# Where the softmax rows of a chunk-attention kernel are normalised: VectorE or ScalarE for the two longer query tiles

## The chip, the cores and the metric

The kernel runs on one core of a Trainium2 chip. The metric is the device time of one execution in microseconds (us), as the median of several runs. A core has several engines that work side by side, each with its own queue of instructions: TensorE (PE in the profile; its weight loads are listed apart as PEld), VectorE (DVE), ScalarE (ACT), GpSimd (POOL) and SyncE (SP), which here only issues DMAs. Each queue is worked off in order; engines wait for one another with semaphores.

## The reference

An input x of 512 frames by 1024 channels goes through two residual layers. Layer 0 has a pooling mixer, layer 1 chunked attention; both are followed by a gated MLP with a causal convolution of width 3. All sub-layers begin with an RMSNorm. What matters here is the attention of layer 1, with 16 heads of 64 channels:

```python
qkv = h @ w_qkv
q, k, v = jnp.split(qkv, 3, axis=-1)
q = head_rmsnorm(q.reshape(B, S, N_HEADS, HEAD_DIM), q_norm)
k = head_rmsnorm(k.reshape(B, S, N_HEADS, HEAD_DIM), k_norm)
...
s = jnp.einsum('bqhd,bkhd->bhqk', qc, kb).astype(jnp.float32) * scale + bias[None]
...
p = jax.nn.softmax(s, axis=-1).astype(vb.dtype)
return jnp.einsum('bhqk,bkhd->bqhd', p, vb)
```

A chunk has 64 frames, and a frame attends to its own chunk and the eight before it, which in a sequence of 512 frames means all earlier chunks and its own.

## The kernel before

All data is float32, and every large matrix product is made of three products of split operands: a value is split into a rounded part (hi, written by ACT with a Copy) and the remainder (lo, a subtraction on DVE, or on POOL where the code asks for it). The helper `split` at lines 91 and 92 does that, `split_scaled` at 96 and 97 the same with a scale, and `mm3` at 112 to 114 issues the three products. Profile rows with L91, L92 or L112 to L114 therefore come from many places; their tile names tell which.

The program is a row of stages: the pooling mixer, the MLP of layer 0 (until about 380 us), the attention (about 380 to 650 us), the MLP of layer 1. PE's order is written out by hand in the attention (`manual_schedule` for PE alone). On the other engines the order is not written out: a planner in the compiler lays the instructions of each queue by times that it works out itself, and so it may place everything anew when an instruction changes its engine.

The attention loop walks over 64 steps: 16 heads h times 4 tiles t of 128 query rows. Because of the causal chunks, tile t only needs the first (t+1) x 128 keys, so tiles 0 to 3 have 128, 256, 384 and 512 columns. Step i does this in PE's order:

- `scores(h, t)` for step i: two matmuls (L661, L662) into PSUM; DVE adds the bias and takes the row minimum of the negated scores (L665); ACT takes the exponential with its row sum (L667); DVE takes the reciprocal of the sum (L668); and the row is multiplied with the reciprocal. For t of 2 and 3 DVE does that (L670, a tensor_scalar), for t of 0 and 1 ACT (L672, a Copy with a scale column).
- `turn(h, t)` for the tile two steps back (LAG is 2): PE transposes the normalised rows (L680, tile tp), then ACT and DVE split the result into the tiles pt.
- `mix(h, m)` two steps later again: the products with V (L695), which ACT and DVE gather into O2 (L699, L700, tile o).
- In two of eight steps `channel_major` for the next pair of heads: transposes of Q or K (L632), then a split on ACT and DVE (L96, L97, or L636 and L639, tile kl), and moves by DMA.

Between these, PE is filled with "fillers": the projections of Q and K for later heads (tile qk), later the output product (tile wo). At the end of each projection a burst of other work comes: ACT reads four PSUM tiles twice (L587, L588), DVE reduces the squares (L589), works out the norm (L590 to L593, tiles qk_a, qk_t, qk_y), and POOL multiplies the four tiles z with it (L595). The split of the weights for fillers has its lo half on POOL (tiles wqk_l and wo_l in L92). POOL also issues the DMA that loads the bias tile B of each head (L655) and writes a corner of it (L656).

When two heads are done, their O2 is split as input of the output product (tile names two<-o). The tiles sb that hold the rows exist four times, as do the small tiles mx for minimum, sum and reciprocal.

Of the kernel before, what the change touches and what calls it, by code (L numbers as in the profile page):

```python
# [19 lines left out]
AF = mybir.ActivationFunctionType  # L20
OP = mybir.AluOpType
# [45 lines left out]
def trunk(ctx: ExitStack, tc: tile.TileContext, xt, xT, cols, band, edge, poolw, gv, wout, wqk, wv, wo, rel, out):  # L67
    nc = tc.nc
# [14 lines left out]
    def psum(tag, name, bufs=2):  # L83
        return ps.tile([P, S], F32, name=name, tag=tag, bufs=bufs)
# [459 lines left out]
    def attention():  # L544
# [103 lines left out]
        def scores(h, t):  # L648

            p, e = divmod(h, 2)  # L650
            q, k, kl = QK[p, 0][e], QK[p, 1][e], KL[p % 2][e]
            if t == 0:
                BT[h] = B = big.tile([P, S], F32, name=f"B{h}", tag="B", bufs=2)
                base = rdram[h, :]
                nc.gpsimd.dma_start(B, bass.AP(tensor=base.tensor, offset=base.offset, ap=[[1, P], [1, S]]))  # L655
                nc.gpsimd.memset(B[:HD, :HD], -NEG)  # L656
            n = (t + 1) * P
            nw = max(n, 256)

            sc = psum("S", f"sc{h}_{t}", 4)  # L660
            nc.tensor.matmul(sc[:, :nw], q[:, t * P:n], k[:, :nw], start=True, stop=False)  # L661
            nc.tensor.matmul(sc[:, :nw], q[:, t * P:n], kl[:, :nw], start=False, stop=True)  # L662
            SM[h, t] = s_ = big.tile([P, S], F32, name=f"sb{h}_{t}", tag="sb", bufs=4)
            mx = tmp.tile([P, 3], F32, name=f"mx{h}_{t}", tag="mx", bufs=4)
            nc.vector.tensor_tensor_reduce(out=s_[:, :n], in0=sc[:, :n], in1=BT[h][:, :n][:, ::-1], scale=1.0,  # L665
                                           scalar=3e38, op0=OP.add, op1=OP.min, accum_out=mx[:, 0:1])
            nc.scalar.activation(s_[:, :n], s_[:, :n], AF.Exp, scale=-1.0, bias=mx[:, 0:1], accum_out=mx[:, 1:2])  # L667
            nc.vector.reciprocal(mx[:, 2:3], mx[:, 1:2])  # L668
            if t > 1:
                nc.vector.tensor_scalar(s_[:, :n], s_[:, :n], mx[:, 2:3], None, op0=OP.mult)  # L670
            else:
                nc.scalar.activation(s_[:, :n], s_[:, :n], AF.Copy, scale=mx[:, 2:3])  # L672

        def turn(h, t):

# [39 lines left out]
        with tc.manual_schedule(engines={mybir.EngineType.PE}):  # L715
# [17 lines left out]
            for i in range(nb + LAG + LAGM):  # L733
                steps = []
                if i < nb:
                    steps.append(lambda: scores(*tiles_[i]))
                if i % 8 in CM and i // 8 + 1 < NPAIR:
                    steps.append(lambda: channel_major(i // 8 + 1, CM.index(i % 8)))
                j = i - LAG
                if 0 <= j < nb:  # L740
                    steps.append(lambda: turn(*tiles_[j]))
                j2 = j - LAGM
                if 0 <= j2 < nb and j2 % 2:
                    steps.append(lambda: mix(tiles_[j2][0], tiles_[j2][1] // 2))
                for x, step in enumerate(steps):
                    step()
                    fill(i + (x + 1) / len(steps))

                while 8 * kept + 7 <= j2 and (cur == 3 or cur == 2 and done >= 24 * (kept // 2 + 1)):
                    split(O2[kept], XS[kept], XS[KD + kept])  # L750
                    kept += 1
# [65 lines left out]
```

## Time and profile before

| | |
|---|---|
| median of 3 runs | 1012.05 us (1011.98 to 1012.12) |
| the profiled execution: time | 1011.85 us |
| the profiled execution: span of its instructions | 1010.1 us |
| mean granted clock of PE in it | 0.997 |
| PE idle from 460 to 640 us | 15.8 us (180.00 less 164.19) |

The span is the time from the first to the last instruction of the program; some 1.8 us of the execution lie around it. The profile's tables are read like this. A row of a timeline has the start in us, the duration in us, the engine, the line of the kernel, the operation, the tiles out<-in, the shape, how many were merged, and in brackets the idle time of the engine before it with what ended that. A row of a group ends in busy us, the mean in ns, and the idle time before. A row of the windows view has, for one stretch of the span, the length and then the busy us of each engine with its count of instructions, then the granted clock of PE (1.00 is full), the share of time in which the DMA engines were busy and GB/s. A row of the waits view has who waited for whom, the us in total, how often, and the longest. The page shows PE's clock and the DMA in 40 slices:

```profile
PEclk9999999999999999999999999999999999999999
DMA  7222323332332234243343333312232342332323
```

Read with the first part of the page, which shows PE nearly always busy, this says that DMA traffic is far from its limit over the whole span.

### The profile page before, as it was taken

The numbers are of one execution on the slowest core, as the hardware profiler recorded it, in microseconds if no ns is written. First come the engines' busy times: TensorE is split into PE (matmuls) and PEld (weight loads), VectorE is DVE, ScalarE is ACT, GpSimd is POOL, SyncE is SP. The second block draws the span as 40 slices with busy tenths as digits, with TensorE's granted clock in tenths as the row PEclk, the third lists the DMA queues.
The fourth block names the chain that finished last, engine by engine and source line by source line (L and its number), as shares of the span: only waits on it lengthen the run. The fifth ranks groups of instructions, "written<-read, shape, count | busy, mean of one in ns | idle before, by whom it ended". The sixth has DMA issues, their size and how long they took to land.

```text
span 1010.1 us, 15577 instructions
## 1 busy us (share of the span) xinstructions
PE 982.3 (97%) x5906; PEld 866.4 (86%) x5906; DVE 820.2 (81%) x1430; ACT 533.5 (53%) x920; POOL 116.4 (12%) x119
## 2 busy tenths in 40 slices
PE   8899999999999999999998889999999999999998
PEld 8678999999999988888777677878999999999986
DVE  7799999988898754443888799989999998989843
ACT  6655544544454443345785767646545454454521
POOL 2400000000000013104524242130000000000000
PEclk9999999999999999999999999999999999999999
DMA  7222323332332234243343333312232342332323
GB/s 288 84 85 82 116 85 109 99 125 95 100 104 82 78 100 146 86 124 115 110 120 83 106 86 92 104 63 97 90 115 98 99 131 90 100 105 86 108 71 112
DMA packets 37290, 105.29 MB, mean 104 GB/s; under 512 B 4416, under 2 KB 6864, under 8 KB 37088
## 3 DMA queue, kind: packets, MB, share of 16 engines
q1 hardware_dynamic: 35728, 99.77, 31.2%
q0 software_dynamic: 1312, 4.24, 1.6%
q8 instruction: 46, 0.75, 0.3%
q10 hardware_dynamic: 176, 0.30, 0.1%
q14 instruction: 28, 0.23, 0.1%
HBM read 95.86 MB, written 2.14 MB: 97 GB/s over the span
## 4 chain that ended last, share of the span: by engine, by line
PE 86%; DVE 8%; ACT 3%; issue 2%; DMA 1%; DVEq 0%; SPq 0%; ACTq 0%
PE out L113 8%; PE out L112 8%; PE out L114 8%; PE st_t L113 6%; PE st_t L112 6%; PE st_t L114 6%; PE st_b L113 5%; PE st_b L112 5%; PE st_b L114 5%; PE gv L113 3%; PE gv L114 3%; PE gv L112 3%; PE qk L114 3%; PE qk L112 3%; PE qk L113 3%
## 5 line engine op out<-in xcount | busy, mean ns | idle before, releaser
L91 ACT ACTIVATE g_h<-gv_r 128x1024 fp32r<-128x1024 f32 x68 | 57.7, 848 | 81.7 <-PE st_t L113 41.0
L113 PE MATMUL out<-one,ow_h 128*128 128x512 f32 x224 | 88.0, 393 | 0.0
L112 PE MATMUL out<-one,ow_h 128*128 128x512 f32 x224 | 87.8, 392 | 0.0
L114 PE MATMUL out<-one,ow_l 128*128 128x512 f32 x224 | 87.7, 392 | 0.0
L91 ACT ACTIVATE ow_h<-wo_r 128x640 fp32r<-128x640 f32 (+1 forms) x64 | 50.5, 789 | 65.2 <-PE out L113 47.3
L511 DVE TENSOR_TENSOR X<-out,X 128x512 f32<-128x512 f32 (+1 forms) x65 | 44.1, 679 | 40.6 <-PE out L114 40.2
L112 PE MATMUL st_t<-h,g_h 128*128 128x256 f32 x272 | 76.9, 283 | 0.0
L114 PE MATMUL st_t<-h,g_l 128*128 128x256 f32 x272 | 76.9, 283 | 0.0
L113 PE MATMUL st_t<-h,g_h 128*128 128x256 f32 x272 | 76.9, 283 | 0.0
L114 PE MATMUL st_t<-two,g_l 128*128 128x256 f32 x272 | 76.5, 281 | 0.0
L113 PE MATMUL st_t<-two,g_h 128*128 128x256 f32 x272 | 76.4, 281 | 0.0
L112 PE MATMUL st_t<-two,g_h 128*128 128x256 f32 x272 | 76.2, 280 | 0.0
L91 ACT ACTIVATE g_h<-sa 128x1024 fp32r<-128x1024 f32 x34 | 36.1, 1060 | 60.2 <-PE st_t L113 42.8
L92 DVE TENSOR_TENSOR g_l<-gv_r,g_h 128x1024 fp32r<-128x1024 f32 x68 | 64.7, 951 | 2.7 <-ACT g_h L91 2.2
L92 DVE TENSOR_TENSOR ow_l<-wo_r,ow_h 128x640 fp32r<-128x640 f32 (+1 forms) x64 | 56.6, 885 | 1.3 <-ACT ow_h L91 1.2
L112 PE MATMUL st_b<-h,g_h 128*128 128x256 f32 x204 | 57.7, 283 | 0.0
L114 PE MATMUL st_b<-h,g_l 128*128 128x256 f32 x204 | 57.7, 283 | 0.0
L113 PE MATMUL st_b<-h,g_h 128*128 128x256 f32 x204 | 57.6, 283 | 0.0
L114 PE MATMUL st_b<-two,g_l 128*128 128x256 f32 x204 | 57.4, 281 | 0.0
L113 PE MATMUL st_b<-two,g_h 128*128 128x256 f32 x204 | 57.3, 281 | 0.0
L112 PE MATMUL st_b<-two,g_h 128*128 128x256 f32 x204 | 57.1, 280 | 0.0
L354 DVE SCALAR_TENSOR_TENSOR c<-a,col,c 128x511 f32<-128x511 f32 (+1 forms) x76 | 56.3, 743 | 0.1
(319 smaller groups left out, 3146.1 us busy)
## 6 DMA issues: line engine op xcount, KB each, us to landing
gv_r<-gv SPq DMA_DIRECT2D x88, 512.0 KB, 3.6
wo_r<-wout SPq DMA_DIRECT2D x32, 384.0 KB, 3.1
wo_r<-wout SPq DMA_DIRECT2D x32, 320.0 KB, 2.9
wqk_r<-wqk SPq DMA_DIRECT2D x16, 512.0 KB, 3.6
wv_r<-wv SPq DMA_DIRECT2D x8, 512.0 KB, 3.5
B<-rdram POOLq DMA_DIRECT2D x16, 256.0 KB, 3.7
wo_r<-wo SPq DMA_DIRECT2D x8, 512.0 KB, 3.5
z<-zh SPq DMA_DIRECT2D x24, 128.0 KB, 2.4
```

The source lines that it names most:

```text
L91: nc.scalar.activation(hi, raw, AF.Copy)
L92: return (eng or nc.vector).tensor_sub(lo, raw, hi.bitcast(F32))
L112: yield nc.tensor.matmul(o, sh, mh, start=first, stop=False)
L113: yield nc.tensor.matmul(o, sh, ml, start=False, stop=False)
L114: yield nc.tensor.matmul(o, sl, mh, start=False, stop=last)
L354: nc.vector.scalar_tensor_tensor(c[:, j:], a[:, :S - j], cw[2 - j], c[:, j:], op0=OP.mult, op1=OP.add)
L511: nc.vector.tensor_add(X[d][:, fs], o[:, fs], X[d][:, fs])
```

## The change

The branch on the tile goes: the multiplication with the reciprocal is a Copy with a scale column on ACT for all four tiles. The reciprocal stays on DVE.

```diff
             nc.scalar.activation(s_[:, :n], s_[:, :n], AF.Exp, scale=-1.0, bias=mx[:, 0:1], accum_out=mx[:, 1:2])
             nc.vector.reciprocal(mx[:, 2:3], mx[:, 1:2])
-            if t > 1:
-                nc.vector.tensor_scalar(s_[:, :n], s_[:, :n], mx[:, 2:3], None, op0=OP.mult)
-            else:
-                nc.scalar.activation(s_[:, :n], s_[:, :n], AF.Copy, scale=mx[:, 2:3])
+            nc.scalar.activation(s_[:, :n], s_[:, :n], AF.Copy, scale=mx[:, 2:3])
```

That is 32 instructions, 16 of 128 x 384 and 16 of 128 x 512 elements, which pass from DVE's queue to ACT's.

## The prediction

> **What bounds the kernel now.** I read the first part of the page, then the windows view cut into the kernel's stages, to see which engine the time belongs to and whether the changed stage holds anything to win.
>
> ```profile
> PE 982.3 (97%) x5906; PEld 866.4 (86%) x5906; DVE 820.2 (81%) x1430; ACT 533.5 (53%) x920; POOL 116.4 (12%) x119
> core 0: us, PE busy (x) PEld busy (x) DVE busy (x) ACT busy (x) POOL busy (x), PEclk, DMA share, GB/s
> 460.00:640.00 180.00, 164.19 (x912) 134.05 (x911) 143.31 (x387) 127.68 (x322) 60.73 (x56) 0.98 0.35 100
> 640.00:730.00 90.00, 89.13 (x447) 75.49 (x447) 85.91 (x130) 52.48 (x79) 12.32 (x7) 1.00 0.28 93
> ```
>
> PE is the bound: 982.3 of 1010.1 us. The softmax steps lie between 460 and 640, and there PE is busy for 164.19 of 180.00, so 15.8 us are idle; DVE has 80% and ACT 71% of the stretch. PE's order is written by hand, so an idle microsecond that goes here goes from the end, unless something behind is late. In the 90 us behind, PE is busy for 89.13; DVE is at 95% there, but its inputs are the sums that the last attention products give, so it moves up with them.
>
> Next, the timelines of DVE and POOL at the largest hole, and that of PE at the four holes that end on a softmax tile.
>
> ```profile
> 569.33 0.49 DVE L670 TENSOR_SCALAR sb<-sb,mx 128x512 f32<-128x512 f32 x1
> 507.25 0.42 DVE L670 TENSOR_SCALAR sb<-sb,mx 128x384 f32<-128x384 f32 x1
> 532.57 6.17 DVE L670 TENSOR_SCALAR sb<-sb,mx 128x512 f32<-128x512 f32 x1
> 582.45 3.78 DVE L670 TENSOR_SCALAR sb<-sb,mx 128x512 f32<-128x512 f32 x1
> 603.22 1.73 DVE L670 TENSOR_SCALAR sb<-sb,mx 128x512 f32<-128x512 f32 x1
> 628.98 1.49 DVE L670 TENSOR_SCALAR sb<-sb,mx 128x512 f32<-128x512 f32 x1
> 532.11 4.04 POOL L595 TENSOR_TENSOR z<-z,qk_y 128x512 f32<-128x512 f32 x4
> 536.11 2.33 POOL L92 TENSOR_TENSOR wqk_l<-wqk_r,wqk_h 128x1024 fp32r<-128x1024 f32 x1
> 539.00 0.55 PE L680 MATMUL tp<-ident,sb 128*128 128x128 f32 x3 [3.94 <-DVE mx L665]
> 586.49 0.66 PE L680 MATMUL tp<-ident,sb 128*128 128x128 f32 x4 [1.78 <-DVE mx L665]
> 605.10 0.63 PE L680 MATMUL tp<-ident,sb 128*128 128x128 f32 x4 [0.69 <-DVE sb L670]
> 630.62 0.63 PE L680 MATMUL tp<-ident,sb 128*128 128x128 f32 x4 [0.46 <-DVE sb L670]
> ```
>
> This is what the changed line costs. L670 takes 0.49 us for 512 columns, but one of them takes 6.17: it starts at 532.57, while POOL is multiplying, and ends at 538.74, 0.3 us after POOL's unbroken run of products and split (536.11 plus 2.33). The others with holes behind them have the same picture. So L670 stands still while POOL works, and everything behind it on DVE with it; the transposes of the softmax tile come late. The releaser that the first two rows name, L665, is the next instruction in DVE's queue, which stood behind the same L670.
>
> **The change, part by part.** It takes 32 instructions L670 from DVE and puts 32 Copies with a scale column on ACT, one per tile of query rows 2 and 3. Reciprocals stay. No DMA is issued or moved. Prices come from the groups by form in 460 to 640, and the clock and the bursts from finer windows:
>
> ```profile
> L670 DVE TENSOR_SCALAR sb<-sb,mx 128x512 f32<-128x512 f32 x16 | 21.3, 1330 | 0.4
> ...
> L670 DVE TENSOR_SCALAR sb<-sb,mx 128x384 f32<-128x384 f32 x16 | 7.7, 482 | 0.3
> ...
> L672 ACT ACTIVATE sb<-sb,mx 128x256 f32<-128x256 f32 x16 | 8.0, 502 | 1.2 <-DVE mx L668 1.2
> ...
> L672 ACT ACTIVATE sb<-sb,mx 128x128 f32<-128x128 f32 x16 | 6.3, 396 | 4.1 <-DVE mx L668 4.0
> 520.00:530.00 10.00, 8.25 (x43) 5.92 (x42) 9.57 (x24) 8.89 (x23) 2.52 (x2) 1.00 0.46 131
> 539.00:545.00 6.00, 6.00 (x27) 5.15 (x28) 3.56 (x11) 4.24 (x12) 0.00 (x0) 0.72 0.27 90
> 565.00:570.00 5.00, 4.92 (x29) 3.44 (x27) 4.72 (x13) 5.00 (x13) 0.56 (x1) 1.00 0.45 126
> 570.00:575.00 5.00, 2.33 (x13) 1.62 (x13) 4.86 (x9) 4.16 (x12) 2.51 (x2) 1.00 0.38 89
> 575.00:580.00 5.00, 4.01 (x13) 2.76 (x13) 3.91 (x14) 2.86 (x9) 0.00 (x0) 0.73 0.33 107
> 590.00:640.00 50.00, 47.10 (x278) 38.82 (x279) 45.94 (x131) 38.85 (x102) 11.31 (x12) 1.00 0.33 96
> ```
>
> Removed from DVE: 21.3 + 7.7 = 29.0 us. Undisturbed it would be 16 x 0.49 + 16 x 0.42 = 14.6, so about 14.4 us are standing still. What counts is the part that PE lost: 3.94 + 1.78 + 0.69 + 0.46 = **6.87 us**. The first hole has a second price: in the 6 us behind it PE has a mean clock of 0.72, and 0.28 x 6 = **1.7 us**. PE stayed busy on the full clock behind the shorter holes at 605 and 630, so I credit this to the long hole and take it as gone. Together 8.6 us.
>
> What is late next at these holes? The same tile's Copy on ACT. ACT's row before it and PE's last matmul before the hole decide:
>
> ```profile
> 531.84 1.05 ACT L91 ACTIVATE wqk_h<-wqk_r 128x1024 fp32r<-128x1024 f32 x1
> 534.66 0.40 PE L113 MATMUL qk<-wqk_l,two 128*128 128x512 f32 x1
> 510.96 0.49 PE L680 MATMUL tp<-ident,sb 128*128 128x128 f32 x3
> ```
>
> At the first hole ACT is free at 532.89, a Copy would end near 533.6, and PE comes for the tile at 535.06: covered by 1.4 us. At the two last holes the tile steps follow each other faster and the margin is smaller: PE lost only 0.69 and 0.46 us to a DVE instruction stretched by 1.2 and 1.0, so the tile's room was some 0.5 us, and a Copy that waits no longer than that closes them too.
>
> Added to ACT: L672 shows 396 ns for 128 columns and 502 for 256, which is 106 per 128 more. Carried on (an estimate from these two rows) that is 0.61 us for 384 and 0.71 for 512, and 16 x 0.61 + 16 x 0.71 = **21.2 us** of work. How much of it delays PE no row shows; the bounds are 0, as long as ACT is idle or the tile has time, and 21.2. Three kinds of place:
> - From 460 to about 590, outside the bursts, the tile has time: the L670 that began at 507.25 ended at 507.67, and its transposes ran at 510.96. A Copy that is 0.2 us longer and queues for one or two more is hidden by those 3.3 us. I take 0.
> - In the bursts, where a projection ends and ACT must read four PSUM tiles twice, ACT has 8.89 of 10 us and 5.00 of 5. Two Copies, 1.3 us, come on top, three times. DVE is relieved of 0.9 us in the same place and is itself at 9.57 of 10. I take 0.7 each, 2.0 us, between 0 and 1.3 each.
> - From 590 on, 12 Copies are 7.9 us, and ACT goes from 38.85 to about 46.8 of 50, that is 94%; DVE falls from 45.94 (12 of the L670, two of them stretched, 7.6 us) to about 38. The two engines change places, and PE lost 2.9 us there with DVE at 92%. Of these, 1.15 are counted above. I take 0.7 us more than now, between 0 and 7.9.
>
> Sum: 8.6 won, 2.7 given back, **5.9 us** less. The profiled execution took 1011.85 us with a span of 1010.1; 1011.85 - 5.9 = 1005.95. The median of 1012.05 is 0.2 above it, so I say **1006.0**.
>
> The Trainium skill has a rule against this change: its page "ScalarE: Activation LUTs" (Rules for kernel authors) puts plain multiplications on VectorE rather than ScalarE. The rows bear that out for one instruction alone, 0.49 us against an estimated 0.71 at 512 columns. By that rule the change would lose 21.2 - 14.6 = 6.6 us where both are on the path, and 1011.85 would become 1018.5; the sum above differs because the row with 6.17 is the same multiplication standing still.
>
> **The rivals.**
> *The load costs nothing and the bursts gain too.* The chain at 571 runs over DVE, which is 4.86 of 5 us busy there:
>
> ```profile
> 569.73 0.74 DVE L639 SCALAR_TENSOR_TENSOR kl<-zt,gq,zh 64x512 fp32r<-64x512 f32 x1
> 571.39 0.35 PE L661 MATMUL sc<-z,z 128*128 128x256 f32 x1 [1.43 <-DVE kl L639]
> ```
>
> L670 stands right before the L639 for which PE waits, so up to 0.4 us goes in each of two bursts, and if the holes at 570 to 577 shrink, the second stretch of slow clock (0.27 x 5 = 1.35 us) goes with them. Then 1012.05 - 8.6 - 0.8 - 1.35 = 1001.3. Against it: ACT is full at that place.
>
> *The standing still moves to another DVE instruction.* Other DVE work meets POOL as well:
>
> ```profile
> L590 DVE TENSOR_TENSOR qk_a<-qk_s,r 128x32 f32<-128x32 f32 x3 | 5.0, 1673 | 0.0
> L92 DVE TENSOR_TENSOR two<-o,two 128x512 fp32r<-128x512 f32 x7 | 4.8, 682 | 0.0
> ...
> L593 DVE TENSOR_TENSOR qk_y<-qk_y,n_y 128x32 f32<-128x32 f32 x3 | 0.5, 182 | 0.0
> ```
>
> L590 and L593 have the same size, and L590 takes nine times as long. The split of the attention output (two<-o) could be caught in the same way if DVE's new order puts it into POOL's run of 4.04 + 2.33 us; none of the 7 is caught now. Price: a hole like that at 535 again, 3.94 + 1.7 = 5.6 us, so 1006.0 + 5.6 = 1011.6. The Trainium skill, "SBUF — State Buffer" (Who interferes with whom), says that a DVE instruction with two SBUF inputs contends with a POOL instruction that reads SBUF, and that the later one waits for the whole of the other; L590 with 1673 ns agrees. By that rule the two<-o split is exposed, and the Copies on ACT are not.
>
> *ACT becomes the bound, and the kernel is slower.* The place is 590 to 640 and the bursts. ACT's queue is in order, and a Copy waits at its head for the reciprocal on DVE; behind it stand the next tile's exponential and the halves of the transposed tiles, for which DVE and PE wait.
>
> ```profile
> ACT sb L672 <- DVE mx L668: 5.2, 10, 1.2
> ```
>
> The 32 Copies of now lost 5.2 us to that wait; as much again, with 7.9 us of late work and 4.0 in the bursts, is 17.1 us if PE sees all of it: 1012.05 - 8.6 + 17.1 = 1020.6. It decides from 8.6 us on, half of that. For it: 94% of ACT's time from 590 on. Against it: DVE at 92% in that same stretch lost PE under 3 us.
>
> **How the numbers follow.** A measurement of this kernel tells about 0.2%, 2 us, from no change, so "same" is 1010.0 to 1014.1. The forecast, 1002.5 to 1010: 0.64. Load free and bursts better, under 1002.5: 0.15. Standing still moved, or half of the ACT load on the path, 1010 to 1014: 0.12. ACT the bound, above 1014: 0.09. Faster 0.79, same 0.12, slower 0.09. The range takes in the free load from 1001.3 and the moved stall up to 1011.6: **1001.0 to 1012.0**.
>
> **What would show it.** Right: in 460 to 640 PE's idle time falls from 15.8 to about 10 us; no hole of over 2 us in front of a transpose; one stretch of slow clock at most; the Copies have means near 0.61 and 0.71; DVE falls by some 25 to 29 us there and ACT rises by about 20. Wrong: a DVE instruction of over 3 us in the stretch, another than L670, means that the stall moved; many waits of transposes or of L91 for ACT after 590 mean that ACT took the bound; a PE idle time that falls while the span doesn't means that the next stage, with DVE at 95%, was late.

## The result, and the profile after

The changed kernel takes 1005.34 us (median of 6 runs, 1004.67 to 1007.35) against 1011.98 us (6 runs, 1011.68 to 1012.12): a ratio of 0.994, interval 0.9927 to 0.9952. That is 6.6 us less, where 5.9 were forecast. The profiled execution took 1005.48 us with a span of 1003.7, 6.4 us less than the span before.

The first part of the page after:

```profile
PE 980.1 (98%) x5906; PEld 867.8 (86%) x5906; DVE 796.7 (79%) x1398; ACT 549.7 (55%) x952; POOL 115.5 (12%) x119
```

The windows view of the same two stages as before; the softmax stage now ends at 634, and the 90 us behind it begin there:

```profile
core 0: us, PE busy (x) PEld busy (x) DVE busy (x) ACT busy (x) POOL busy (x), PEclk, DMA share, GB/s
460.00:634.00 174.00, 162.78 (x915) 136.00 (x914) 120.36 (x356) 144.39 (x354) 59.79 (x56) 0.97 0.37 105
634.00:724.00 90.00, 89.13 (x448) 75.70 (x449) 85.94 (x129) 52.11 (x79) 12.30 (x7) 1.00 0.30 93
```

The stage is 6 us shorter. PE's idle time in it falls from 15.8 us to 174.00 - 162.78 = 11.2, and its busy time by 1.4. DVE loses 143.31 - 120.36 = 23.0 us and ACT gains 16.7 (the window is 6 us shorter too). The next stage hides nothing and takes nothing: 89.13 of 90.00, as before. So nearly the whole gain, 6.0 of 6.4 us, comes from where it was looked for. What is left of the idle time is not where it was looked for.

The groups by form in the softmax stage, with busy us and mean ns behind the bar:

```profile
L669 ACT ACTIVATE sb<-sb,mx 128x512 f32<-128x512 f32 x16 | 11.4, 716 | 0.3 <-DVE mx L668 0.3
L669 ACT ACTIVATE sb<-sb,mx 128x384 f32<-128x384 f32 x16 | 9.8, 609 | 0.6 <-DVE mx L668 0.5
```

The waits view of the stage: who waits for whom, us in total, how often, the longest:

```profile
PE tp L677 <- ACT sb L669: 8.9, 6, 3.3
```

And PE's timeline at the two longest of these waits:

```profile
527.65 1.11 PE L677 MATMUL tp<-ident,sb 128*128 128x128 f32 x4 [3.34 <-ACT sb L669]
572.84 0.66 PE L677 MATMUL tp<-ident,sb 128*128 128x128 f32 x4 [2.71 <-ACT sb L669]
```

The Copies (L669 now) cost 716 and 609 ns, 21.2 us in all. The hole of 3.94 us that L670 had made is gone, and no DVE instruction in the stage lasts over 2 us. But the transposes of the softmax tile (L677 now) wait 8.9 us for the Copy, and two of these waits are 3.34 and 2.71 us long. Both come before the four transposes of a 512-column tile, both at a projection's end. The timelines of ACT, DVE and POOL ahead of the first one show the chain:

```profile
518.40 0.68 DVE L665 CUSTOM_DVE_ANT_0 sb<-sc,B 128x512 f32<-128x512 f32 x1
522.45 1.14 ACT L91 ACTIVATE wqk_h<-wqk_r 128x1024 fp32r<-128x1024 f32 x1
523.66 0.81 ACT L667 ACTIVATE sb<-sb,mx 128x512 f32<-128x512 f32 x1
523.75 2.35 POOL L92 TENSOR_TENSOR wqk_l<-wqk_r,wqk_h 128x1024 fp32r<-128x1024 f32 x1
524.32 1.82 DVE L590 TENSOR_TENSOR qk_a<-qk_s,r 128x32 f32<-128x32 f32 x1
526.49 0.15 DVE L668 RECIPROCAL mx<-mx 128x1 f32<-128x1 f32 x1
526.89 1.00 ACT L669 ACTIVATE sb<-sb,mx 128x512 f32<-128x512 f32 x2
```

The minimum of the row is there at about 519.1, but the exponential runs at 523.66, behind the burst's squares and copies and the weight split of 1.14 us. Its sum is ready at about 524.6; by then DVE is inside L590, which lies beside POOL's weight split and takes 1.82 us. The reciprocal follows at 526.49, the Copy at 526.89, and PE, which had finished at 524.3, begins at 527.65. ACT's queue, DVE's queue and POOL's split beside it stand in a row here, and the Copy itself is the shortest part. In the kernel before, ACT's timeline has the same exponential 3.5 us earlier, 2.0 us after its minimum:

```profile
520.18 0.78 ACT L667 ACTIVATE sb<-sb,mx 128x512 f32<-128x512 f32 x1
```

So the planner's new order of ACT's queue, and not the length of the Copies, is the longest part of the chain.

The windows view around this hole shows PE's clock behind it:

```profile
524.00:527.00 3.00, 0.31 (x2) 0.00 (x0) 2.97 (x7) 2.95 (x11) 2.10 (x1) 0.82 0.22 47
527.00:530.00 3.00, 2.35 (x8) 2.06 (x9) 2.04 (x9) 2.09 (x5) 0.00 (x0) 0.50 0.62 189
530.00:533.00 3.00, 3.00 (x13) 2.62 (x11) 1.71 (x6) 0.78 (x2) 2.20 (x3) 0.54 0.00 0
```

In the 6 us that follow, the granted clock is 0.50 and 0.54, as it was below full behind the largest hole of before.

### The profile page after: what moved, and what is told of

It is laid out like the page before. It is cut to its first block, busy times and chain, and to the rows that moved or that the text cites. A ratio compares the mean times of both kernels' runs of the same rounds, so it can differ in the third digit from the quotient of the medians.

```text
span 1003.7 us, 15609 instructions
## 1 busy us (share of the span) xinstructions
PE 980.1 (98%) x5906; PEld 867.8 (86%) x5906; DVE 796.7 (79%) x1398; ACT 549.7 (55%) x952; POOL 115.5 (12%) x119
## 4 chain that ended last, share of the span: by engine, by line
PE 86%; DVE 6%; ACT 5%; DMA 1%; issue 1%; SPq 0%; DVEq 0%; ACTq 0%
PE out L113 8%; PE out L112 8%; PE out L114 8%; PE st_t L113 6%; PE st_t L112 6%; PE st_t L114 6%; PE st_b L113 5%; PE st_b L112 5%; PE st_b L114 5%; PE gv L113 3%; PE gv L114 3%; PE gv L112 3%; PE qk L114 3%; PE qk L112 3%; PE qk L113 3%; PE oo L692 2%
```

## The experiments

Two questions were open. Was it the standing still of L670 that the change removed, or simply DVE's load? And what did the 21.2 us of Copies cost? Times are medians; each ratio is to the kernel before, run beside it, with its interval in brackets. The kernel before had medians of 1011.88 to 1012.14 us in these runs, and single runs from 1010.63 to 1015.51, so two kernels whose intervals overlap are not told apart by their medians.

### The multiplication stays on DVE, in a form that isn't held up

From the kernel before; the second operation adds zero, and the row's sum goes to a column that nobody reads:

```diff
-            mx = tmp.tile([P, 3], F32, name=f"mx{h}_{t}", tag="mx", bufs=4)
+            mx = tmp.tile([P, 4], F32, name=f"mx{h}_{t}", tag="mx", bufs=4)
...
-                nc.vector.tensor_scalar(s_[:, :n], s_[:, :n], mx[:, 2:3], None, op0=OP.mult)
+                nc.vector.tensor_scalar(s_[:, :n], s_[:, :n], mx[:, 2:3], 0.0, op0=OP.mult, op1=OP.add, accum_out=mx[:, 3:4])
```

> The kernel before, with the 32 multiplications left on DVE, but as a tensor_scalar that also writes its row sum (unused). Theory A (the gain is that DVE no longer stands still behind POOL): if this form does not stand still, the holes of PE at 535, 582, 603 and 628 close although DVE has more work (estimated from 128x384 and 128x512 DVE rows of 0.55 and 0.69 us and accumulator reads of 0.08: 7.8 us more than undisturbed), so 1004 to 1008 us, and no L670 longer than 1 us. Theory B (the gain is that DVE, at 92% from 590 on, lost 14.6 us of work): DVE gets fuller, so 1012 to 1016 us. If the form stands still as well, L670 again has a maximum of several us and the time is 1012 or more, and A and B are not told apart by it.

Measured: **1001.03 us**, 0.9889 [0.9872, 0.9906], the lowest median of all kernels here, and 3 us below the range that theory A gave. The groups by form of this kernel:

```profile
L670 DVE TENSOR_SCALAR_CACHE_REDUCE sb<-sb,mx 128x512 f32<-128x512 f32 x16 | 11.9, 742 | 0.4
L670 DVE TENSOR_SCALAR_CACHE_REDUCE sb<-sb,mx 128x384 f32<-128x384 f32 x16 | 9.8, 610 | 0.3
```

Its timeline of POOL and DVE where one of them meets POOL:

```profile
531.01 2.05 POOL L595 TENSOR_TENSOR z<-z,qk_y 128x512 f32<-128x512 f32 x2
531.57 0.75 DVE L670 TENSOR_SCALAR_CACHE_REDUCE sb<-sb,mx 128x512 f32<-128x512 f32 x1
```

And its window of the stage:

```profile
460.00:629.40 169.40, 161.61 (x913) 133.53 (x911) 134.37 (x420) 128.19 (x322) 60.22 (x56) 0.99 0.38 107
```

The new form is dearer than an undisturbed L670 (742 ns against 490), and yet the kernel gains 10.9 us. The row at 531.57 is the tile that had stood still for 6.17 us before: it begins 0.56 us after POOL's products do and takes its usual 0.75. In the whole stage nine of the 32 begin inside a run of POOL, and none of the 32 takes over 0.75 us; in the kernel before eight of the 32 began so, and each of the eight ended 0.2 to 0.3 us after POOL's run. DVE's work in the stage falls only from 143.31 to 134.37, far less than in the changed kernel, and without standing still the new form is the heavier load (21.7 us against 14.6). PE's idle time is 169.40 - 161.61 = 7.8 us. So it was the standing still and not the load. The Trainium skill, "SBUF — State Buffer" (Who interferes with whom), excepts the form of tensor_scalar that also writes out its accumulator from those that can contend with GpSimd; the row at 531.57 agrees.

This kernel also gives one way to take the change's two terms apart. It has the stall removed and nothing new on ACT. From before to here: 10.9 us; from here to the changed kernel: 1005.34 - 1001.03 = 4.3 us given back, and the two intervals do not overlap. The planner ordered the queues of the two kernels differently, so the 4.3 us are what the Copies and that order cost together.

### Only one of the two tiles moves

Three kernels: 512 columns on ACT and 384 on DVE as before; 384 on ACT and 512 on DVE as before; 384 on ACT and 512 on DVE in the sum form (with the tile mx one column wider, as above).

```diff
-            if t > 1:
+            if t == 2:
```

> Only the tiles with 512 columns go to ACT; those with 384 stay on DVE. All four holes of PE that ended on a stretched L670 belonged to 512 columns. Theory A: nearly the whole gain, with 11.4 instead of 21.2 us of Copies on ACT, so 1003 to 1006 us. Theory B: 8 of 14.6 us of DVE work are gone, so a bit over half the gain, about 1008.3 us.

```diff
-            if t > 1:
+            if t == 3:
```

> Only the tiles with 384 columns go to ACT; those with 512 stay on DVE. Theory A: the stretched 512 ones stay, so within 2 us of the kernel before, 1010 to 1013 us, with an L670 of over 3 us. Theory B: 6.7 of 14.6 us of DVE work are gone, so a bit under half the gain, about 1009 us, with the holes of PE smaller everywhere rather than the same.

```diff
-            if t > 1:
-                nc.vector.tensor_scalar(s_[:, :n], s_[:, :n], mx[:, 2:3], None, op0=OP.mult)
+            if t > 2:
+                nc.vector.tensor_scalar(s_[:, :n], s_[:, :n], mx[:, 2:3], 0.0, op0=OP.mult, op1=OP.add, accum_out=mx[:, 3:4])
```

> Tiles with 384 columns on ACT, those with 512 on DVE in the form with a row sum. It stands between the run with all 32 on DVE in that form (1001.03 us) and the changed kernel. If that form is free of standing still and the rest is a matter of load, 1000 to 1003.5 us; if the order that the planner makes decides more than the load, anything from 999 to 1006 us.

Measured: **1004.57** (0.9922 [0.9907, 0.9936]), **1006.11** (0.994 [0.9927, 0.9954]) and **1001.65** (0.9904 [0.9888, 0.9919]).

With 512 alone on ACT the time is nearly that of the changed kernel, and so are the holes before the transposes: 3.26 us at 526.79 and 3.66 at 571.81, both ended by the Copy.

In the second kernel, with 512 on DVE as before, the group of L670 by form:

```profile
L670 DVE TENSOR_SCALAR sb<-sb,mx 128x512 f32<-128x512 f32 x16 | 15.3, 954 | 0.4
```

And its timeline of POOL and DVE at the longest of them:

```profile
575.85 4.04 POOL L595 TENSOR_TENSOR z<-z,qk_y 128x512 f32<-128x512 f32 x4
576.03 4.15 DVE L670 TENSOR_SCALAR sb<-sb,mx 128x512 f32<-128x512 f32 x1
```

The expectation of the second, that the full price of the stall would stay, was a miss. Its 16 instructions take 15.3 us in place of 21.3, and the one of 6.17 us isn't among them: moving the other half changed the planner's order. Six still began inside a run of POOL, but only one of them, of 4.15 us, stood still from nearly the first product of a long run to its last; the others took 1.69 us at most. What a stall costs is thus set by which instruction happens to meet POOL, and when, not by the line alone.

The third splits what was given back: 1001.65 lies inside the spread of the sum form on both tiles, and the two ratios' intervals overlap, so the 16 Copies of 384 columns cost little (0.6 us by the medians), and those of 512 columns the rest, 3.7 us. In its waits view the transposes wait only 1.5 us for a Copy, as against 8.9 in the changed kernel:

```profile
PE tp L680 <- ACT sb L672: 1.5, 3, 0.6
```

### Is it DVE's L590 in the burst?

The hole at 527.65 had L590 in its chain. Two kernels take it out: the squares get a scale column in L587, and L590 and the epsilon of the head norm (L591) are left out in the later projections. The first is built on the changed kernel, the second on the sum form.

```diff
-                nc.scalar.activation(sq, ov[t], AF.Square)
+                nc.scalar.activation(sq, ov[t], AF.Square, **({"scale": r8[:, t:t + 1]} if c else {}))
...
+            if c:
+                rsqrt(ss, y, t_)
+            else:
...
```

> The changed kernel without L590 in the later projections: its factor goes into the scale column of the square on ACT (L587), and the epsilon of the head norm is left out there. It asks what makes the two holes of 3.34 and 2.71 us that the changed kernel has in the bursts at 524 and 570. Theory C (DVE stands still at L590 behind POOL's wqk_l or wo_l split for about 1.7 us, the reciprocal behind it is late, and the Copy with it): the holes shrink by 1.5 us or more each and the slow clock behind them shrinks, so 1000 to 1003 us. Theory D (ACT's queue alone is late, since the exponential of the tile begins 4.5 us after its minimum): within 1 us of the changed kernel, 1004.3 to 1006.3 us, holes as they are.

> All 32 multiplications on DVE in the form with a row sum, and L590 taken out of the later projections as in the run with the folded factor (the epsilon of the head norm is left out there). With the multiplications off ACT, L590's standing still (0.88, 1.18 and 1.18 us) lies in a burst whose holes end on DVE (tile kl) and on what follows L590. If DVE is what is late there, 1 to 3 us less than 1001.03: 998 to 1000 us. If it is ACT, or PE's order, 1000 to 1002 us.

A third, built on the changed kernel, puts the three Copies that follow a projection's end (tile 3 of heads 0, 4 and 8) back on DVE in the sum form.

```diff
-            nc.scalar.activation(s_[:, :n], s_[:, :n], AF.Copy, scale=mx[:, 2:3])
+            if (h, t) in ((0, 3), (4, 3), (8, 3)):
+                nc.vector.tensor_scalar(s_[:, :n], s_[:, :n], mx[:, 2:3], 0.0, op0=OP.mult, op1=OP.add, accum_out=mx[:, 3:4])
+            else:
+                nc.scalar.activation(s_[:, :n], s_[:, :n], AF.Copy, scale=mx[:, 2:3])
```

> The changed kernel with three of the 32 multiplications back on DVE, in the form that also writes its row sum: those of (head, tile) (0,3), (4,3) and (8,3), the ones whose Copy ended just ahead of PE's waiting transposes in the bursts. Theory D (the holes of 0.84, 3.34 and 2.71 us come from the Copy's place in ACT's queue): the two large holes fall under 1.6 us each and the slow clock behind them goes or shrinks, so 1000 to 1003 us. Otherwise (the exponential or the reciprocal of these tiles is late in any case) the holes stay over 2.5 us and the time is within 1 us of the changed kernel, 1004.3 to 1006.3 us.

Measured: **1007.08** (0.9949 [0.9936, 0.9962]), **1002.08** (0.9896 [0.9881, 0.9911]) and **1004.36** (0.9922 [0.9908, 0.9935]). None brings the gain that its theory named. The first is slower than both of its ranges, and all three holes in front of its 512-column transposes are a little longer than in the changed kernel (1.46, 3.44 and 2.92 us for 0.84, 3.34 and 2.71); why it is slower stays open. The second ends just above its upper range. The third falls where its alternative put it: both large holes stay, 3.29 and 2.71 us. The timelines of ACT, DVE and PE at the hole, on the changed kernel without L590:

```profile
524.50 0.80 ACT L671 ACTIVATE sb<-sb,mx 128x512 f32<-128x512 f32 x1
525.42 0.16 DVE L672 RECIPROCAL mx<-mx 128x1 f32<-128x1 f32 x1
527.72 0.71 ACT L673 ACTIVATE sb<-sb,mx 128x512 f32<-128x512 f32 x1
528.48 0.33 PE L681 MATMUL tp<-ident,sb 128*128 128x128 f32 x1 [3.44 <-ACT sb L673]
```

The same timelines in the kernel with this tile's multiplication on DVE:

```profile
522.04 0.81 ACT L667 ACTIVATE sb<-sb,mx 128x512 f32<-128x512 f32 x1
522.70 1.95 DVE L590 TENSOR_TENSOR qk_a<-qk_s,r 128x32 f32<-128x32 f32 x1
525.17 0.75 DVE L670 TENSOR_SCALAR_CACHE_REDUCE sb<-sb,mx 128x512 f32<-128x512 f32 x1
525.98 1.12 PE L680 MATMUL tp<-ident,sb 128*128 128x128 f32 x4 [3.29 <-DVE sb L670]
```

Without L590 the reciprocal is early, at 525.58, and the Copy then stands 2.1 us in ACT's queue; with the multiplication on DVE, L590 is what it stands behind. Each engine's queue is long enough to make the hole when the other's is cut. What both share is the start: an exponential that runs late, 5.0 and 4.6 us after its minimum, where the kernel before had 2.0.

### What a microsecond of ACT's work costs

To double the load, 32 more Copies of 128 x 384 into a tile that nobody reads go into the changed kernel, first from a constant tile without a scale, then with the row's reciprocal as scale, which ties each to its step.

```diff
             nc.scalar.activation(s_[:, :n], s_[:, :n], AF.Copy, scale=mx[:, 2:3])
+            if t > 1:
+                junk = big.tile([P, 384], F32, name=f"junk{h}_{t}", tag="junk", bufs=1)
+                nc.scalar.activation(junk, set1[0].bitcast(F32)[:, :384], AF.Copy)
```

> The changed kernel with 32 more Copies on ACT, one behind each of the moved ones: 128x384 from a tile that nobody writes then into a scratch tile that nobody reads. It measures what ACT's load is worth: 32 times 0.61 us, 19.5 us, close to the 21.2 us of the change. If ACT hides its load as the prediction had it (2.7 of 21.2 us on the path), 1007 to 1010 us. If ACT is the bound of the bursts and of the stretch from 590 on (theory D), the second load is hidden worse than the first, and 10 us or more come on top: above 1015 us.

```diff
-                nc.scalar.activation(junk, set1[0].bitcast(F32)[:, :384], AF.Copy)
+                nc.scalar.activation(junk, set1[0].bitcast(F32)[:, :384], AF.Copy, scale=mx[:, 2:3])
```

> The changed kernel with 32 more Copies on ACT, one per tile of query rows 2 and 3, as in the run with more load, but now each takes the tile's reciprocal as its scale column, so that it cannot run before the softmax of its tile (in the earlier run all 32 ran between 434 and 462 us, ahead of the attention loop). 19.5 us of added work among the tiles. If ACT hides its load as the prediction had it (2.7 of 21.2 us on the path), 1007 to 1010 us. If ACT is the bound in the bursts and from 590 on, 10 us or more come on top: above 1015 us.

Measured: **1004.7** (0.9929 [0.9915, 0.9942]) and **1008.97** (0.9966 [0.9954, 0.9979]). The first tells nothing: as they hung on no tile, the planner put all 32 between 434.3 and 462.3, ahead of the loop. In the second they run in the loop, as its groups by form show:

```profile
L672 ACT ACTIVATE junk<-one,mx 128x384 f32<-128x384 f32 x32 | 19.4, 608 | 0.0
```

The window of its stage:

```profile
460.00:640.00 180.00, 166.60 (x928) 137.73 (x927) 123.73 (x360) 159.10 (x389) 59.94 (x56) 0.97 0.36 101
```

19.4 us more on ACT cost 1008.97 - 1005.34 = 3.6 us, 0.19 us for each, within the range expected of a mostly hidden load. The change's own 21.2 us cost 4.3 by the sum form, which is 0.20. As each difference is uncertain by more than 1 us, this says about a fifth and no more. Even with 159.10 of 180 us on ACT, four fifths of the work are hidden.

### The exponential first

In the changed kernel, the burst's later instructions are ordered behind the exponential of the tile just scored: the last two pairs of squares and copies, the split zh, the second part of the next weights wqk, and in the first kernel the first split of wo as well.

```diff
-                hi, lo = load_split(w[kk], 1024, f"{name}_{kk}", eng=eng)
+                with tc.issue_after(last[1].ins) if 1 in last and kk == 1 else nullcontext():
+                    hi, lo = load_split(w[kk], 1024, f"{name}_{kk}", eng=eng)
...
-                nc.scalar.activation(sq, ov[t], AF.Square)
-                nc.scalar.activation(z.rearrange("p h d -> p (h d)"), ov[t], AF.Copy)
+                with tc.issue_after(last[0].ins) if last and t > 1 else nullcontext():
+                    nc.scalar.activation(sq, ov[t], AF.Square)
+                    nc.scalar.activation(z.rearrange("p h d -> p (h d)"), ov[t], AF.Copy)
...
-                nc.scalar.activation(zh, zt, AF.Copy, scale=gq[:, i:i + 1])
+                with tc.issue_after(last[0].ins) if last else nullcontext():
+                    nc.scalar.activation(zh, zt, AF.Copy, scale=gq[:, i:i + 1])
```

> The changed kernel with edges for ACT's order alone: in the burst at the end of a projection, the square and copy of its last two PSUM tiles, the split of K (zh) and the next weights' split are queued behind the exponential of the tile that was just scored. Theory E (the holes of 3.34 and 2.71 us come from this exponential, which the changed kernel's order puts behind the whole burst, at 523.66 though its minimum was there at 519.08): the exponential runs some 2 us earlier, the reciprocal passes ahead of L590, the two holes fall under 1.6 us each, 1000 to 1003 us. If instead ACT's load itself makes the holes, they stay or move to another wait in the burst, and the time is 1004 us or more.

> As the run with edges for ACT's order, but without the edge on the split of the first output weights (wo): in that run PE waited 4.39 us for this split at 561, a hole that the edge itself made. Theory E: the hole at 561 goes, that in the burst at 524 stays at 1.4 us or less instead of 3.34, that at 570 falls under 1.6 us instead of 2.71, and the time is 1001 to 1004 us. If the holes come back elsewhere in the bursts, 1004 us or more: then the sum of the ACT and DVE work in the burst makes them, and not the place of the one exponential.

Measured: **1008.41** (0.9962 [0.9949, 0.9974]) with the edge on wo, **1004.25** (0.9927 [0.9913, 0.994]) without it. ACT's and PE's timelines of the first:

```profile
520.03 0.77 ACT L672 ACTIVATE sb<-sb,mx 128x512 f32<-128x512 f32 x1
525.56 0.33 PE L682 MATMUL tp<-ident,sb 128*128 128x128 f32 x1 [1.36 <-ACT sb L674]
565.41 0.80 PE L112 MATMUL wo<-two,wo_h 128*128 128x512 f32 x1 [4.39 <-ACT wo_h L91]
```

With the exponential at 520.03 the hole of 3.34 us shrinks to 1.36; the edge on wo then made a new one of 4.39 at a split for which PE waits. Without that edge, the first hole is 1.36 us as well, and PE's timeline has these:

```profile
565.79 0.35 PE L665 MATMUL sc<-z,z 128*128 128x256 f32 x1 [1.41 <-DVE kl L644]
568.27 0.47 PE L681 MATMUL tp<-ident,sb 128*128 128x128 f32 x1 [1.55 <-ACT sb L673]
609.43 0.50 PE L665 MATMUL sc<-z,z 128*128 128x512 f32 x1 [1.12 <-DVE mx L669]
```

And the windows of its stage, of the first burst and of the second:

```profile
460.00:632.50 172.50, 161.21 (x913) 133.56 (x911) 120.04 (x355) 143.97 (x354) 59.91 (x56) 0.99 0.37 105
520.00:535.00 15.00, 13.31 (x76) 10.80 (x75) 12.81 (x36) 14.53 (x36) 5.74 (x7) 1.00 0.38 105
560.00:580.00 20.00, 17.02 (x96) 14.15 (x95) 15.68 (x48) 18.28 (x45) 8.95 (x9) 0.91 0.35 93
```

The large holes are gone, but PE's idle time is 172.50 - 161.21 = 11.3 us, as in the changed kernel: it is spread over shorter holes. The medians differ by 1005.34 - 1004.25 = 1.1 us, which the overlapping intervals don't confirm; PE's busy time is shorter by 1.6 us (162.78 to 161.21), with a mean clock of 0.99 in place of 0.97. In the first burst the clock stays full where it was 0.50; in the second a slow stretch remains. By the expectation, holes of this size belong to theory E, but a time of 1004 us or more to the other theory, that the work of the burst as a whole makes the holes. So, with the exponential put ahead of that work, the large holes shrink, and at the first the slow clock goes; the sum of the idle time doesn't.

One of the new holes has another cause. The timelines of DVE and POOL ahead of the one at 609.43:

```profile
606.23 2.66 DVE L92 TENSOR_TENSOR two<-o,two 128x512 fp32r<-128x512 f32 x1
605.97 2.38 POOL L92 TENSOR_TENSOR wo_l<-wo_r,wo_h 128x1024 fp32r<-128x1024 f32 x1
```

The split of the attention output, 0.69 us elsewhere, stands still here beside POOL's split of the weights, and the row minimum for which PE waits 1.12 us is queued behind it. In the kernel with the edge on wo one such split takes 2.54 us.

The kernel with the sum form has the exponential early without any edge, as ACT's timeline shows:

```profile
519.30 0.78 ACT L667 ACTIVATE sb<-sb,mx 128x512 f32<-128x512 f32 x1
```

Its hole there is 1.18 us, at 522.73, and the stage holds only 7.8 us of idle time. Why the order in the burst is better there, and why the rest of the idle time in the last kernel moved rather than went, was not settled: no run had the sum form with the exponential put late.

## Why the prediction was right, and where it wasn't

The time, 1006.0 predicted and 1005.34 measured, is right, and so is the mechanism in its outline: the standing still goes, most of the Copies is hidden, and something is given back in the bursts. That the total came so close is in part luck. Measured against the sum form both terms were too small, by 2.3 and 1.6 us, and the two errors cancel; inside the load's term, two bursts were off in opposite ways.

**The stall: predicted 8.6 us, 10.9 by the sum form.** The step was "6.87 us" of PE's lost time and "1.7 us" of slow clock. The sum form takes PE's idle time from 15.8 to 7.8, that is 8.0 us, and its busy time from 164.19 to 161.61, 2.6 us. Its instruction is the dearer one, so the stall alone may be worth more still; its queues are ordered anew too, so this is no strict bound. The predicted sum counted four holes and the clock behind one of them. That it left the second slow stretch, at 575, out was right: the sum form still has one, with a clock of 0.66 from 570 to 575. No hole ahead of that stretch is over 1.48 us, so slow clock doesn't belong to single long holes alone, as the sum had it.

**The load on ACT: predicted 2.7 us, 4.3 by the sum form.** The prices of 0.61 and 0.71 us were right to 6 ns or so (609 and 716), and so was the sum of 21.2. The step that failed is "Two Copies, 1.3 us, come on top, three times ... I take 0.7 each": it priced the length of the Copies and took the order of ACT's queue as it was. What happened in the bursts is that a tile's steps pass from ACT to DVE and to ACT again, each time to the end of a full queue that the planner had laid anew. The late exponential led to a hole of 3.34 us at one place and 2.71 at another, with slow clock behind.

The profiles of before and after give a second division, without a third kernel. The windows of the two later bursts, two from before and two from after, and the stretch to the stage's end after:

```profile
515.00:545.00 30.00, 24.32 (x130) 19.37 (x129) 26.52 (x60) 20.55 (x52) 10.35 (x10) 0.94 0.28 80
565.00:590.00 25.00, 19.06 (x98) 13.96 (x96) 22.08 (x54) 16.92 (x44) 9.20 (x10) 0.93 0.28 75
515.00:535.00 20.00, 16.29 (x79) 13.08 (x78) 14.91 (x39) 15.53 (x39) 7.07 (x7) 0.83 0.36 102
565.00:585.00 20.00, 16.54 (x92) 13.59 (x91) 16.86 (x47) 17.78 (x44) 9.25 (x10) 0.91 0.32 87
585.00:634.00 49.00, 46.29 (x281) 38.69 (x280) 39.35 (x119) 44.43 (x113) 10.81 (x12) 1.00 0.35 98
```

Less the four holes of L670, PE's idle time in the burst at 525 rises from 30.00 - 24.32 - 3.94 = 1.7 to 3.7 us, and in the one at 570 it falls from 25.00 - 19.06 - 1.78 = 4.2 to 3.5. The bound "between 0 and 1.3 each" was therefore no bound: one burst lies above it and one below. The first burst and all else up to 515 give nothing (53.71 of 55.00 busy before, 53.66 after). From there to the stage's end the idle time was 2.90 - 1.15 = 1.75 and is 49.00 - 46.29 = 2.71, so 1.0 more where 0.7 was forecast. Together 2.3 us of idle time are given back, near the 2.7, and PE's busy time falls by 1.4 us where 1.7 of slow clock were to go. By this division the sums were nearly right and the places in the bursts wrong.

**The signs.** "PE's idle time falls from 15.8 to about 10 us": 11.2. The prediction's own terms give 15.8 - 6.87 + 2.7 = 11.6, since its 1.7 us of slow clock are busy time and not idle time. "DVE falls by some 25 to 29 us there and ACT rises by about 20": 23.0 and 16.7, in a window that is 6 us shorter. "No hole of over 2 us in front of a transpose" and "one stretch of slow clock at most" were wrong, both through the same two holes. The signs against it did not come: no DVE instruction of over 3 us, and after 590 three waits of transposes for a Copy, 0.96 us at most.

**The rivals.** That the load costs nothing and the bursts gain did not come; 1001.3 was its time, and the sum form, which adds no load on ACT, came out at 1001.03. That the stall moves to another DVE instruction did not come in the changed kernel: the split of the attention output (two<-o) has 684 ns after and 682 before. It did come in the two kernels with edges, where one such split was caught, for 2.54 and 2.66 us. L590, 1787 ns for 1673, matters only as one link of the chain in the burst. That ACT becomes the bound was far off: at 0.19 us per microsecond of work, the 21.2 us cost about 4 us, half of the 8.6 from which it would have decided.

The rule of the Trainium skill, "ScalarE: Activation LUTs" (Rules for kernel authors), that plain multiplications belong on VectorE, was set aside in the prediction because the multiplication stood still there. With a form that doesn't, it holds here: the kernel is 4.3 us faster with it on VectorE, though one instruction has nearly the same price (742 and 716 ns).

## What to carry to other kernels

When one instruction of a group takes ten times its usual time, look at what runs beside it before you move the group: the same engine may have a form that isn't held up, whereas moving the work away trades the stall for a load elsewhere. Price a moved instruction by the chain it stands in, not by its length: where queues are full, each hand-over between engines can cost a wait in the queue, and a planner may order the queue anew. A load that is added evenly can be mostly hidden (a fifth of it was seen here), so look for the one place where it isn't.

## What the hardware showed beyond that

In the kernel before and in the one with 384 columns on ACT, the standing still of L670 lasted, but for one case, as long as POOL's unbroken run and not one instruction of it: 4.15 us beside four products of 4.04 in all, and 6.17 beside four such products and a split. The one case is in the latter kernel, as its timelines of DVE and POOL show:

```profile
533.24 0.71 DVE L670 TENSOR_SCALAR sb<-sb,mx 128x512 f32<-128x512 f32 x1
533.63 1.22 POOL L595 TENSOR_TENSOR z<-z,qk_y 128x512 f32<-128x512 f32 x1
```

This L670 began inside the first of four products, took only 0.71 us, and it was the second product that took longer, 1.22 us where the kernel before has 1.06 at most. In the kernel with 512 columns on ACT, one at 532.26 passed in a like way, in 0.89 us. What let them in between is open.
